# A third block of gate and up by seven products, and down with both column halves open, in a two-block transformer kernel on one Trainium2 core

## The chip, the core and the metric

The kernel runs on one core of one Trainium2 chip. The metric is the device time of one execution in microseconds, the median of several runs. The engines are named as in the profile: TensorE (PE, its weight loads PEld), VectorE (DVE), ScalarE (ACT), GpSimd (POOL) and SyncE (SP), which only issues DMAs.

## What is computed

Two transformer blocks on 256 tokens of width 1024, all in float32. The first block is a feed-forward stage, a mixer (top-k sparse attention beside a pooled branch) and a feed-forward stage; the second is a feed-forward stage, a gated mixer and a feed-forward stage, with a norm at the end. Cut to what the change touches:

```python
def swiglu(x, w_gate, w_up, w_down):          # w_gate, w_up 1024 x 2816; w_down 2816 x 1024
    return (jax.nn.silu(x @ w_gate) * (x @ w_up)) @ w_down

x = x + 0.5 * swiglu(rms_norm(x, g), w_gate, w_up, w_down)     # four times in all

q = rope(rms_norm(q.reshape(B, S, 8, 64), q_norm), pos, 64)    # first mixer; k likewise

return rmsnorm(x, final_norm)                                  # the end
```

## The kernel before

**Products.** Each float32 operand is split into a high and a low half that TensorE takes at full rate: ScalarE writes the high half (`whi`, L80), DVE subtracts it for the low half (`wlo`, L81). `mm3` (L83) makes one product of three matmuls: high by high (L86), high by low (L87), low by high (L88). A weight block is 128 x 2048 numbers, four k-tiles by 512 columns, 1 MB. It is loaded by SP's queue into one of two `raw` buffers or by POOL's queue into one of four `block` buffers of the stage, and split into one of three `whi`/`wlo` pairs. A block is used by 24 matmuls (2 token tiles x 4 k-tiles x 3), in the order of the token tiles.

**A feed-forward stage** (`ffn`, L322) has gate and up in six column blocks j = 0 to 5, the last one half as wide. `eight(j)` (L348) makes a block of gate and of up from four weight blocks, 96 matmuls. `seven(j)` (L362) makes the same by seven products of 12 matmuls each (`quad`, L157): four of the weight blocks' sums and differences are made, two by accumulating DMAs (L178), two on DVE (L196, L199, at the sixth and the seventh product), and the results are put together from the products by additions on DVE (L191, L197, L202 to L205, L367). The products go to the three PSUM banks of `tmp`. Every seven loads four weight blocks and accumulates two, splits seven, and takes all four `block` buffers in turn.

Behind a block come silu (L334) and the product with up (L342); `turned` (L208) then transposes it on TensorE and splits it into `act`, the operand of down.

`down` (L372) makes the two column halves f = 0 and 1 of the output one after the other, each over 22 k-tiles in five weight blocks (c = 0 to 4) and one of half size (c = 5). `add` (L254) puts a half into X, takes the squares for the next norm, and queues the transposes of X (L274) and the two halves of `hT` (L226, L227), the operand of the next stage; `later` and `flush` place them some steps on.

**Order.** `ORDER` (L36) is a string with a letter for each step of a stage, behind block 0: `a` and `b` are products of the two sevens (7 each), `2` and `4` the weight blocks of the two eights (4 each), `e` those of the half block (2), `d` those of down. The order of instructions on an engine, and the waits, are made by a scheduler from this order and the tiles' uses, so neighbours on an engine can change places.

**Elsewhere.** In the first mixer `mixer1_tables` (L426) loads constants and the gains `q_norm` and `k_norm` and makes with them on DVE the rope tables of q and k (L440, L443). `heads` (L520) uses these later. Behind the last stage, `run` (L853 to L870) loads the final gain `fg`, sums the squares, takes the inverse root on POOL (L101), multiplies and stores.

Of the kernel before, what the change touches and what calls it, by code (L numbers as in the profile page):

```python
# [10 lines left out]
F32 = mybir.dt.float32  # L11
F32R = mybir.dt.float32r
AF = mybir.ActivationFunctionType
ALU = mybir.AluOpType
# [3 lines left out]
P = 128  # L18
T = 256
D = 1024  # L20
KD = D // P
FF = 2816
KF = FF // P
HD = 64
NH = 8
# [7 lines left out]
MASKED = -1.0e30  # L33
WARM = 14

ORDER = "eeaa2a2aa2a2a44bb4b4bbdbdbdddddddddd"  # L36


class Block:
# [214 lines left out]
    def add(self, accs, f, scale, following, tiles=(0, 1)):  # L254
# [23 lines left out]
        for k in (4 * f, 4 * f + 2):  # L278
            self.later(lambda k=k: pair(k), 3)


    def warm_up(self):

# [38 lines left out]
    def ffn(self, n, following, first=False):  # L322
        nc, a = self.nc, self.a
        gu, d, d_end = a[f"gu{n}"], a[f"d{n}"], a[f"de{n}"]
        with self.stage(4), self.tc.tile_pool(name="act", bufs=1) as pool:
            act = pool.tile([P, KF, 2, T], F32R, tag="act", name="act")
            xc = pool.tile([P, 16, 2, P], F32R, tag="xc", name="xc")
            r = None

            def silu(gs):  # L330
                sgs = []
                for t in range(2):
                    sg = self.work.tile([P, 512], F32, tag="sg", name="sg")[:, : gs[t].shape[1]]
                    nc.scalar.activation(sg, gs[t], AF.Silu, scale=r[:, t : t + 1])  # L334
                    sgs.append(sg)
                return sgs

            def gated(j, sgs, us):
                prs = []
                for t in range(2):  # L340
                    pr = self.work.tile([P, 512], F32, tag="pr", name="pr", bufs=4)[:, : us[t].shape[1]]
                    nc.vector.scalar_tensor_tensor(pr, us[t], r[:, t : t + 1], sgs[t], op0=ALU.mult, op1=ALU.mult)  # L342
                    prs.append(pr)
                self.later(lambda: self.turned(act, prs, 4 * j), 4)

            two = lambda: [self.bank("acc") for _ in range(2)]

            def eight(j):  # L348
                G = two()
                self.token_major(G, gu[2 * j], 512, 0)  # L350
                yield
                self.token_major(G, gu[2 * j], 512, 1)
                sgs = silu([x[:, :T] for x in G] if j == 5 else G)
                if j < 5:
                    yield
                    U = two()
                    self.token_major(U, gu[2 * j + 1], 512, 0)
                    yield
                    self.token_major(U, gu[2 * j + 1], 512, 1)
                gated(j, sgs, [x[:, T:] for x in G] if j == 5 else U)  # L360

            def seven(j):  # L362
                y11, y21, y12, x, y22 = yield from self.quad(pool, [[gu[2 * j + i, c] for i in range(2)] for c in range(2)], self.hT, xc)

                def rest():
                    tt = nc.vector.tensor_tensor
                    tt(y12, y12, x, op=ALU.add)  # L367
                    gated(j, silu([y11, y21]), [y12, y22])

                self.later(rest, 3)  # L370

            def down():  # L372
                for f in range(2):
                    accs = two()
                    w = lambda c: self.weights(d[f, c] if c < 5 else d_end[f])
                    rows = lambda c, w, last, **k: self.rows(accs, w, act, 4 * c, 4 if c < 5 else 2, last, **k)
                    split = f == 1 and following == "final_norm_2"
                    order = (0, 1, 2, 4, 5, 3) if f == 0 else range(4 if split else 6)
                    for c in order:
                        if f or c:  # L380
                            yield
                        rows(c, w(c), 15 if f == 0 else KF - 1)
                    if split:
                        ws = [w(4), w(5)]
                        for t in range(2):
                            for c in (4, 5):
                                rows(c, ws[c - 4], KF - 1, tiles=[t])
                            self.add(accs, f, 0.5, following, [t])
                    else:
                        self.add(accs, f, 0.5, following)  # L390


            G, U = two(), two()
            if first:
                self.cold_start((G, U), gu)
            else:
                self.token_major(G, gu[0], 512, 0)
                self.flush()
                self.token_major(U, gu[1], 512, 0)
                self.flush()  # L400
                self.token_major(G, gu[0], 512, 1)
            r = self.rstd()
            if not first:
                self.token_major(U, gu[1], 512, 1)
            gated(0, silu(G), U)
            combined = self.combined(xc, self.hT)
            next(combined)

            steps = {"a": seven(1), "b": seven(3), "2": eight(2), "4": eight(4), "e": eight(5), "d": down()}
            for step in ORDER:  # L410
                next(steps[step], None)
                self.flush(1 if step in "ab" else 2)
                next(combined, None)

    def rope(self, dst, src, C, S, heads, half):
# [10 lines left out]
    def mixer1_tables(self):  # L426
        nc, a, c1 = self.nc, self.a, self.c1
        load = lambda name, shape, engine=None: self.load(c1, name, shape, engine)
        self.cosi, self.sini = load("cosi", [P, 2, 32]), load("sini", [P, 2, 32])
        cosq, sinq = load("cosq", [P, 2, 64]), load("sinq", [P, 2, 64])  # L430
        self.causal, self.ncausal = load("causal", [P, 2, T], nc.gpsimd), load("ncausal", [P, 2, T], nc.gpsimd)
        self.band, self.pw = load("band", [P, 4, 384], nc.gpsimd), load("pool_w", [P, 4, P], nc.gpsimd)
        self.pscale = load("pool_scale", [P, 4], nc.gpsimd)
        self.tabs = {}
        for n in ("q", "k"):
            g = c1.tile([P, HD], F32, tag=f"{n}g", name=f"{n}g")
            nc.sync.dma_start(g, a[f"{n}_norm"].to_broadcast([P, HD]))
            C = c1.tile([P, 2, HD], F32, tag=f"{n}C", name=f"{n}C")
            S = c1.tile([P, 2, HD], F32, tag=f"{n}S", name=f"{n}S")
            nc.vector.tensor_tensor(C, cosq, g[:, None, :].to_broadcast([P, 2, HD]), op=ALU.mult)  # L440
            for i in range(2):
                o, s = slice(i * 32, i * 32 + 32), slice(32 - i * 32, 64 - i * 32)
                nc.vector.tensor_tensor(S[:, :, o], sinq[:, :, o], g[:, None, s].to_broadcast([P, 2, 32]), op=ALU.mult)  # L443
            self.tabs[n] = (C, S)

    def mixer1(self, following):
        nc, a = self.nc, self.a
# [71 lines left out]

        def heads(n):  # L520
            rs, ros = [], []
            for t in range(2):
                src = accs[n][t].rearrange("p (h d) -> p h d", d=HD)
                ss = self.small.tile([P, NH], F32, tag="ss8", name="ss8")
# [3 lines left out]
                r = self.small.tile([P, NH], F32, tag=f"r8{n}", name="r8")  # L528
                self.rsqrt(r, ss, rr[:, t : t + 1])
                ro = self.m1.tile([P, NH, HD], F32, tag="ro", name="ro", bufs=2)  # L530
                self.rope(ro, src, self.tabs[n][0][:, t, :], self.tabs[n][1][:, t, :], NH, 32)
                nc.vector.tensor_scalar(r, r, rt[:, t : t + 1], HD ** -0.5 if n == "q" else 1.0, op0=ALU.mult, op1=ALU.mult)
                if n == "k":
                    for h in range(NH):
# [298 lines left out]
    def run(self):  # L833
# [16 lines left out]
            self.mixer2("ffn2_norm_2")  # L850
        self.ffn(4, "final_norm_2")

        fg = self.raw.tile([P, 2048], F32, tag="raw", name="fg")[:, :D]  # L853
        nc.sync.dma_start(fg, a["final"].to_broadcast([P, D]))
        for t in range(2):
            y = self.raw.tile([P, 2048], F32, tag="raw", name="y")[:, :D]
            tot = self.small.tile([P, 1], F32, tag="tot1", name="tot")
            nc.vector.tensor_tensor(tot, self.sq[:, 0, t : t + 1], self.sq[:, 1, t : t + 1], op=ALU.add)
            r = self.small.tile([P, 1], F32, tag="r1", name="r1")
            self.rsqrt(r, tot, 1.0 / D)  # L860
            for f in range(2):
                s = slice(f * 512, f * 512 + 512)
                nc.vector.tensor_tensor(y[:, s], self.X[t][:, s], fg[:, s], op=ALU.mult)
            for f in range(2):
                s = slice(f * 512, f * 512 + 512)
                if f:
                    nc.vector.tensor_scalar(y[:, s], y[:, s], r, None, op0=ALU.mult)
                else:
                    nc.scalar.activation(y[:, s], y[:, s], AF.Copy, scale=r)
                (nc.scalar if f == 0 and t == 1 else nc.sync).dma_start(self.out[t * P : t * P + P, s], y[:, s])  # L870

def _constants():
# [92 lines left out]
```

## Time and profile before

| what | us |
|---|---|
| median of 3 runs | 1085.7 (1085.14 to 1086.57) |
| the profiled execution | 1086.12 |
| its span in the trace | 1084.3 |
| TensorE busy | 1064.9 |
| DVE busy | 758.4 |
| ScalarE busy | 576.4 |

All times of the trace are microseconds from the span's start. Matmuls are pipelined: how long one takes says less than how far apart two of them start. "Idle before" is the time for which an engine had nothing to do before an instruction, followed by who ended it. The granted clock (PEclk) is the share of TensorE's full clock. The stages lie in the trace so: feed-forward up to 192 us, first mixer to 297, feed-forward to 479, feed-forward to 662, second mixer to 894, feed-forward to 1075, the end.

### The profile page before, as it was taken

How to read it: one execution, taken by the hardware profiler on the slowest of the kernel's cores; microseconds unless marked ns; L12 is line 12 of the kernel's file. 1: busy time of each engine (PE TensorE's matmuls, PEld its weight loads, DVE VectorE, ACT ScalarE, POOL GpSimd, SP SyncE). 2: the span in 40 equal slices, each digit the busy share in tenths (PEclk: the TensorE clock that was granted, in tenths of full speed). 3: DMA queues.
4: the chain of work that ended last, by engine and by line, in shares of the span. 5: the costliest groups of instructions: out<-in, count | busy, mean ns of one | idle time of the engine just before them, and what ended most of it. 6: DMA issues, size and time to landing. Idle time of an engine off the chain costs nothing.

```text
span 1084.3 us, 12898 instructions
## 1 busy us (share of the span) xinstructions
PE 1064.9 (98%) x5182; PEld 893.0 (82%) x5182; DVE 758.4 (70%) x780; ACT 576.4 (53%) x657; POOL 51.0 (5%) x85
## 2 busy tenths in 40 slices
PE   9899999899999999999999999999999999999996
PEld 8688888778888888888888878999888888888885
DVE  7788874697586969547788665777555467796953
ACT  7656543577456564545656345534444445556541
POOL 0100000120010000001000000000000001000000
PEclk9999999899999999999999999999999999999998
DMA  9976365633298643559773655454455438865361
GB/s 356 328 238 206 117 233 191 236 117 118 89 321 250 251 138 142 207 193 337 245 233 117 253 204 204 160 204 174 171 186 194 155 126 301 271 239 150 130 217 61
DMA packets 34955, 218.54 MB, mean 202 GB/s; under 512 B 4608, under 2 KB 5008, under 8 KB 10320
## 3 DMA queue, kind: packets, MB, share of 16 engines
q1 hardware_dynamic: 26784, 164.20, 41.4%
q0 software_dynamic: 7680, 52.98, 16.7%
q8 instruction: 40, 0.66, 0.2%
q10 hardware_dynamic: 432, 0.55, 0.1%
q14 instruction: 19, 0.16, 0.0%
HBM read 216.66 MB, written 1.05 MB: 201 GB/s over the span
## 4 chain that ended last, share of the span: by engine, by line
PE 92%; DMA 5%; DVE 1%; ACT 1%; issue 1%; SPq 0%; POOLq 0%; POOL 0%; ACTq 0%; DVEq 0%
PE acc L88 21%; PE acc L87 21%; PE acc L86 20%; PE tmp L86 8%; PE tmp L88 8%; PE tmp L87 8%; PE tmp L214 2%; DMA raw<-in_gu 1%; PE acc L94 1%; DMA block<-in_gu 1%; DVE wlo L81 1%; DMA qg<-in_q_norm 1%; DMA raw<-in_de 1%; PE tmp L274 1%; PE tmp L94 1%
## 5 line engine op out<-in xcount | busy, mean ns | idle before, releaser
L81 DVE TENSOR_TENSOR wlo<-raw,whi 128x2048 fp32r<-128x2048 f32 (+1 forms) x127 | 282.2, 2222 | 157.2 <-ACT whi L80 156.9
L80 ACT ACTIVATE whi<-raw 128x2048 fp32r<-128x2048 f32 (+1 forms) x127 | 236.5, 1862 | 210.9 <-PE acc L88 123.7
L81 DVE TENSOR_TENSOR wlo<-block,whi 128x2048 fp32r<-128x2048 f32 (+2 forms) x99 | 198.8, 2014 | 71.4 <-ACT whi L80 71.4
L80 ACT ACTIVATE whi<-block 128x2048 fp32r<-128x2048 f32 (+2 forms) x99 | 167.2, 1694 | 118.7 <-PE acc L88 59.9
L87 PE MATMUL acc<-wlo,hT 128*128 128x512 f32 (+1 forms) x560 | 218.6, 390 | 3.3 <-DVE wlo L81 3.3
L88 PE MATMUL acc<-whi,hT 128*128 128x512 f32 (+1 forms) x560 | 218.0, 390 | 3.2 <-DVE hT L227 3.2
L86 PE MATMUL acc<-whi,hT 128*128 128x512 f32 (+1 forms) x560 | 218.8, 392 | 0.0
L86 PE MATMUL acc<-whi,act 128*128 128x512 f32 x352 | 138.3, 393 | 0.6 <-ACT whi L80 0.5
L87 PE MATMUL acc<-wlo,act 128*128 128x512 f32 x352 | 136.9, 390 | 0.4 <-DVE wlo L81 0.4
L88 PE MATMUL acc<-whi,act 128*128 128x512 f32 x352 | 135.9, 389 | 0.0
L87 PEld LDWEIGHTS acc<-wlo,hT 128*128 128x128 f32 x560 | 106.1, 189 | 25.5 <-DVE wlo L81 4.4
L88 PEld LDWEIGHTS acc<-whi,hT 128*128 128x128 f32 x560 | 106.1, 189 | 24.6 <-DVE hT L227 3.5
L86 PEld LDWEIGHTS acc<-whi,hT 128*128 128x128 f32 x560 | 106.2, 190 | 21.9 <-ACT hT L226 0.5
L86 PEld LDWEIGHTS acc<-whi,act 128*128 128x128 f32 x352 | 66.1, 188 | 15.1 <-ACT act L80 1.3
L87 PEld LDWEIGHTS acc<-wlo,act 128*128 128x128 f32 x352 | 66.1, 188 | 14.8 <-DVE wlo L81 1.5
L88 PEld LDWEIGHTS acc<-whi,act 128*128 128x128 f32 x352 | 66.1, 188 | 13.9
L86 PE MATMUL tmp<-whi,hT 128*128 128x512 f32 x192 | 75.8, 395 | 0.0
L88 PE MATMUL tmp<-whi,hT 128*128 128x512 f32 x192 | 74.8, 390 | 0.0
L87 PE MATMUL tmp<-wlo,hT 128*128 128x512 f32 x192 | 74.8, 389 | 0.0
L86 PE MATMUL tmp<-whi,xc 128*128 128x512 f32 x128 | 50.2, 392 | 1.0 <-ACT p L175 1.0
L88 PE MATMUL tmp<-whi,xc 128*128 128x512 f32 x128 | 49.9, 390 | 0.0
L87 PE MATMUL tmp<-wlo,xc 128*128 128x512 f32 x128 | 49.8, 389 | 0.0
(264 smaller groups left out, 1380.0 us busy)
## 6 DMA issues: line engine op xcount, KB each, us to landing
raw<-in_gu SPq DMA_DIRECT2D x52, 1024.0 KB, 6.7
block<-in_gu POOLq DMA_DIRECT2D x48, 1024.0 KB, 8.3
raw<-in_d SPq DMA_DIRECT2D x40, 1024.0 KB, 4.8
raw<-in_de SPq DMA_DIRECT2D x8, 512.0 KB, 3.5
block<-in_w_out SPq DMA_DIRECT2D x4, 1024.0 KB, 4.9
raw<-in_w_out SPq DMA_DIRECT2D x4, 1024.0 KB, 5.6
block<-in_w_cx SPq DMA_DIRECT2D x4, 1024.0 KB, 5.0
raw<-in_w_cx SPq DMA_DIRECT2D x4, 1024.0 KB, 5.0
```

The source lines that it names most:

```text
L80: self.nc.scalar.activation(hi, x, AF.Copy)
L81: self.nc.vector.tensor_tensor(lo, x, hi.bitcast(F32), op=ALU.subtract)
L86: mm(ps, lhsT=a[0], rhs=b[0], start=start, stop=False)
L87: mm(ps, lhsT=a[0], rhs=b[1], start=False, stop=False)
L88: mm(ps, lhsT=a[1], rhs=b[0], start=False, stop=stop)
L94: self.nc.tensor.matmul(ps, lhsT=a, rhs=b, start=start, stop=stop)
L214: self.nc.tensor.transpose(pt[:, i, :], x[t][:, i * P : i * P + P], self.ident)
L274: nc.tensor.transpose(pt[:, i, t * P : t * P + P], self.X[t][:, (k + i) * P : (k + i) * P + P], self.ident)
```

## The change

In every feed-forward stage block 2 is made by seven products too, so that blocks 1, 2 and 3 are `a`, `b` and `c`, and the eights are 0, 4 and the half block. `ORDER` starts with the half block and block 4 among `a`, then puts blocks of down among `b` and `c`. For this `down` opens both column halves at once (four PSUM banks) and goes through the weight blocks in the order `DOWN`, pairs of half and k-block: k-blocks 0, 5 and 4 of both halves first, then 1, 2 and 3. The last weight block is done by token tile. The half f = 0 is added to X at the block before the last.

The rope tables of q and k are made on DVE in `heads`, where they are used; their loads stay where they were. The end loads `fg` and multiplies the first column half with it when that half is ready, makes half of the variance ahead, and does the rest of each token tile behind its part of the last weight block, with both queues for the stores.

```diff
-ORDER = "eeaa2a2aa2a2a44bb4b4bbdbdbdddddddddd"
+ORDER = "eeaa4aa4a4aa4bbdbbdbbdbccdccdcdcdcdddddd"
+DOWN = ((0, 0), (0, 5), (0, 4), (1, 0), (1, 5), (1, 4), (0, 1), (1, 1), (0, 2), (1, 2), (0, 3), (1, 3))
...
+    def ending(self):
...
+        self.fg = self.block()[:, :D]
+        nc.sync.dma_start(self.fg, self.a["final"].to_broadcast([P, D]))
+        self.half = self.small.tile([P, 2], F32, tag="tot", name="half")
+        nc.vector.tensor_scalar(self.half, self.sq[:, 0, :], 1.0 / D, EPS, op0=ALU.mult, op1=ALU.add)
+        self.y = [self.block()[:, :D] for _ in range(2)]
+        for t in range(2):
+            nc.vector.tensor_tensor(self.y[t][:, :512], self.X[t][:, :512], self.fg[:, :512], op=ALU.mult)
+
+    def finish(self, t):
+        nc, y = self.nc, self.y[t]
+        v = self.small.tile([P, 1], F32, tag="tot1", name="v")
+        nc.vector.scalar_tensor_tensor(v, self.sq[:, 1, t : t + 1], 1.0 / D, self.half[:, t : t + 1], op0=ALU.mult, op1=ALU.add)
+        r = self.small.tile([P, 1], F32, tag="r1", name="r1")
+        nc.gpsimd.tensor_tensor(r, v, self.mhalf[:, :1], op=ALU.pow)
+        nc.vector.tensor_tensor(y[:, 512:], self.X[t][:, 512:], self.fg[:, 512:], op=ALU.mult)
+        nc.scalar.activation(y[:, :512], y[:, :512], AF.Copy, scale=r)
+        nc.vector.tensor_scalar(y[:, 512:], y[:, 512:], r, None, op0=ALU.mult)
+        for f, queue in ((0, nc.scalar), (1, nc.sync)):
+            s = slice(f * 512, f * 512 + 512)
+            queue.dma_start(self.out[t * P : t * P + P, s], y[:, s])
...
-                self.later(lambda: self.turned(act, prs, 4 * j), 4)
+                self.later(lambda: self.turned(act, prs, 4 * j), 2 if j == 3 else 4)
...
             def down():
...
+                accs = [two(), two()]
+                for f, c in DOWN:
+                    if (f, c) != DOWN[0]:
+                        yield
+                    w = self.weights(d[f, c] if c < 5 else d_end[f])
+                    rows = lambda tiles: self.rows(accs[f], w, act, 4 * c, 4 if c < 5 else 2, 15, tiles=tiles)
+                    if (f, c) != DOWN[-1]:
+                        rows((0, 1))
+                        if c == 3:
+                            self.add(accs[f], f, 0.5, following)
+                            if following == "final_norm_2":
+                                self.ending()
+                        continue
+                    for t in range(2):
+                        if t:
+                            yield
+                        rows([t])
+                        if following == "final_norm_2":
+                            self.add(accs[f], f, 0.5, following, [t])
+                            self.finish(t)
+                    if following != "final_norm_2":
+                        self.add(accs[f], f, 0.5, following)
...
-            steps = {"a": seven(1), "b": seven(3), "2": eight(2), "4": eight(4), "e": eight(5), "d": down()}
+            steps = {"a": seven(1), "b": seven(2), "c": seven(3), "4": eight(4), "e": eight(5), "d": down()}
             for step in ORDER:
                 next(steps[step], None)
-                self.flush(1 if step in "ab" else 2)
+                self.flush(1 if step in "abc" else 2)
...
-        self.tabs = {}
+        self.heads_of = {}
         for n in ("q", "k"):
...
-            nc.vector.tensor_tensor(C, cosq, g[:, None, :].to_broadcast([P, 2, HD]), op=ALU.mult)
...
+            self.heads_of[n] = (cosq, sinq, g)
+
+    def tables_of(self, n):
...
         def heads(n):
             rs, ros = [], []
+            C, S = self.tables_of(n)
```

## Rows read from the trace of the kernel before

**Rows 1.** The page's first part: busy time, share of the span, instructions of each engine.
```profile
PE 1064.9 (98%) x5182; PEld 893.0 (82%) x5182; DVE 758.4 (70%) x780; ACT 576.4 (53%) x657; POOL 51.0 (5%) x85
```

**Rows 2.** Timeline of TensorE (start, us, what): first matmuls of two neighbouring products of b.
```profile
404.64 0.39 PE L86 MATMUL tmp<-whi,hT 128*128 128x512 f32 x1
...
407.36 0.39 PE L86 MATMUL tmp<-whi,xc 128*128 128x512 f32 x1
```

**Rows 3.** The list of TensorE's waits: us in total, times, longest us; the two largest.
```profile
PE acc L87 <- DVE wlo L81: 3.7, 3, 1.7
PE acc L88 <- DVE hT L227: 3.2, 1, 3.2
```

**Rows 4.** Table of stretches of the second feed-forward stage: us, busy us of each engine.
```profile
core 0: us, PE busy (x) PEld busy (x) DVE busy (x) ACT busy (x) POOL busy (x), PEclk, DMA share, GB/s
303.00:330.00 27.00, 27.00 (x122) 22.33 (x121) 21.65 (x18) 15.42 (x14) 4.03 (x7) 1.00 1.01 353
405.00:430.00 25.00, 25.00 (x116) 20.78 (x115) 23.88 (x19) 13.92 (x11) 0.00 (x0) 1.00 0.30 106
```

**Rows 5.** Timeline of DVE in that stretch, operations one behind the other.
```profile
404.70 2.28 DVE L196 TENSOR_TENSOR block<-block 128x2048 f32<-128x2048 f32 x1
...
407.56 0.68 DVE L191 TENSOR_TENSOR p<-tmp,p 128x512 f32<-128x512 f32 x1
408.16 2.28 DVE L81 TENSOR_TENSOR wlo<-raw,whi 128x2048 fp32r<-128x2048 f32 x1
410.36 2.29 DVE L81 TENSOR_TENSOR wlo<-block,whi 128x2048 fp32r<-128x2048 f32 x1
```

**Rows 6.** Timeline of TensorE: first use of the low half that started at 408.16.
```profile
411.19 0.40 PE L87 MATMUL acc<-wlo,act 128*128 128x512 f32 x1
```

**Rows 7.** The page's DMA issues: count, KB each, us from issue to landing.
```profile
block<-in_gu POOLq DMA_DIRECT2D x48, 1024.0 KB, 8.3
```

**Rows 8.** Timeline of TensorE: the transposes of X's first column half, second stage.
```profile
453.09 1.03 PE L274 MATMUL tmp<-ident,X 128*128 128x128 f32 x8
```

**Rows 9.** Timeline of DVE: the low halves of `hT` made from them.
```profile
457.45 0.87 DVE L227 SCALAR_TENSOR_TENSOR hT<-tmp,gains,hT 128x256 fp32r<-128x256 f32 x2
458.47 0.88 DVE L227 SCALAR_TENSOR_TENSOR hT<-tmp,gains,hT 128x256 fp32r<-128x256 f32 x2 [0.15 <-ACT hT L226]
```

**Rows 10.** Timeline of DVE in the first mixer: the first table and the next low half.
```profile
201.43 0.29 DVE L440 TENSOR_TENSOR qC<-cosq,qg 128x128 f32<-128x128 f32 x1 [4.54 <-DMA qg<-in_q_norm]
...
202.39 2.28 DVE L81 TENSOR_TENSOR wlo<-raw,whi 128x2048 fp32r<-128x2048 f32 x1
```

**Rows 11.** Timeline of TensorE in the first mixer: bounds of w_idx's two weight blocks.
```profile
191.54 0.31 PE L86 MATMUL acc<-whi,hT 128*128 128x324 f32 x1
...
195.10 1.04 PE L274 MATMUL acc<-ident,X 128*128 128x128 f32 x8
...
201.46 0.31 PE L86 MATMUL acc<-whi,hT 128*128 128x324 f32 x1
...
211.12 0.39 PE L86 MATMUL tmp<-whi,hT 128*128 128x512 f32 x1
```

**Rows 12.** Table of stretches, columns as in rows 4: the stop there and behind it.
```profile
201.40:205.10 3.70, 0.52 (x3) 0.21 (x2) 3.67 (x9) 0.00 (x0) 0.00 (x0) 0.83 0.98 406
205.10:210.60 5.50, 5.48 (x19) 5.24 (x20) 4.04 (x8) 3.19 (x4) 0.00 (x0) 0.50 0.63 220
```

**Rows 13.** Timeline of DVE in the tail, second token tile.
```profile
1076.74 0.16 DVE L858 TENSOR_TENSOR tot<-sq 128x1 f32<-128x1 f32 x1 [0.85 <-ACT junk L233]
...
1077.64 0.15 DVE L100 TENSOR_SCALAR var<-tot 128x1 f32<-128x1 f32 x1
1077.70 0.68 DVE L863 TENSOR_TENSOR y<-X,fg 128x512 f32<-128x512 f32 x1
```

**Rows 14.** Timeline of POOL in the tail: the inverse roots of both token tiles.
```profile
1073.10 0.56 POOL L101 TENSOR_TENSOR r<-var,mhalf 128x1 f32<-128x1 f32 x1 [94.69 <-DVE var L100]
1077.86 0.93 POOL L101 TENSOR_TENSOR r<-var,mhalf 128x1 f32<-128x1 f32 x1 [4.21 <-DVE var L100]
```

More of the change, by code (lines that the diff above doesn't have):

```diff
@@ L279, in add @@
             self.later(lambda k=k: pair(k), 3)
+    def ending(self):
+        nc = self.nc
+        self.fg = self.block()[:, :D]
[17 more added lines that the diff above has]
+            queue.dma_start(self.out[t * P : t * P + P, s], y[:, s])
     def warm_up(self):
@@ L372, in down @@
             def down():
[L373 to L380, printed above, removed]
-                            yield
[L382 to L390, printed above, removed]
+                accs = [two(), two()]
[13 more added lines that the diff above has]
+                        if t:
+                            yield
+                        rows([t])
[4 more added lines that the diff above has]
+                        self.add(accs[f], f, 0.5, following)
             G, U = two(), two()
@@ L437, in mixer1_tables @@
             nc.sync.dma_start(g, a[f"{n}_norm"].to_broadcast([P, HD]))
-            C = c1.tile([P, 2, HD], F32, tag=f"{n}C", name=f"{n}C")
-            S = c1.tile([P, 2, HD], F32, tag=f"{n}S", name=f"{n}S")
-            nc.vector.tensor_tensor(C, cosq, g[:, None, :].to_broadcast([P, 2, HD]), op=ALU.mult)
[L441 to L444, printed above, removed]
+            self.heads_of[n] = (cosq, sinq, g)
+    def tables_of(self, n):
+        nc, (cosq, sinq, g) = self.nc, self.heads_of[n]
+        C = self.c1.tile([P, 2, HD], F32, tag=f"{n}C", name=f"{n}C")
+        S = self.c1.tile([P, 2, HD], F32, tag=f"{n}S", name=f"{n}S")
+        nc.vector.tensor_tensor(C, cosq, g[:, None, :].to_broadcast([P, 2, HD]), op=ALU.mult)
+        for i in range(2):
+            o, s = slice(i * 32, i * 32 + 32), slice(32 - i * 32, 64 - i * 32)
+            nc.vector.tensor_tensor(S[:, :, o], sinq[:, :, o], g[:, None, s].to_broadcast([P, 2, 32]), op=ALU.mult)
+        return C, S
     def mixer1(self, following):
@@ L530, in heads @@
                 ro = self.m1.tile([P, NH, HD], F32, tag="ro", name="ro", bufs=2)
-                self.rope(ro, src, self.tabs[n][0][:, t, :], self.tabs[n][1][:, t, :], NH, 32)
+                self.rope(ro, src, C[:, t, :], S[:, t, :], NH, 32)
                 nc.vector.tensor_scalar(r, r, rt[:, t : t + 1], HD ** -0.5 if n == "q" else 1.0, op0=ALU.mult, op1=ALU.mult)
@@ L851, in run @@
         self.ffn(4, "final_norm_2")
[L853 to L870, printed above, removed]
 def _constants():
```

## The prediction

> **What bounds the kernel now.** I read the page's busy shares first: TensorE is busy 98% of the span, VectorE (DVE) 70% [rows 1]. Matmuls are pipelined, so a busy share alone proves little; the start times settle it. Twelve matmuls of 512 columns, one product of the seven, start 2.72 us apart from the next product's twelve [rows 2]: 0.227 us each, and a weight block of 24 takes 5.44 us. The list of TensorE's waits then adds to about 10 us in all; its two largest entries are 3.7 us on DVE's low halves (`wlo`) and one wait of 3.2 us on a low half of `hT` [rows 3]. So TensorE sets the time nearly everywhere, and a matmul taken out is worth its 0.227 us, if what feeds TensorE keeps up.
>
> What feeds it is DVE: each weight block needs its low half from DVE, and only three pairs `whi`/`wlo` exist, so a block's split can't start before the matmuls of the third block before it are done. The table of stretches shows the second feed-forward stage: at its densest, 405 to 430 us, DVE is busy 23.88 of 25.00 us while TensorE is busy throughout; from 303 to 330 us, near the stage's start, the DMA engines move 353 GB/s [rows 4].
>
> **1. Twelve matmuls fewer per stage.** A block of gate and up by eight products is 4 x 24 = 96 matmuls, by seven 7 x 12 = 84. One block more in four stages: 48 x 0.227 = **-10.9 us**, all on the path.
>
> **2. What the third seven adds on DVE.** Three more low halves, two more sums of weight blocks and some eight operations of 512 elements per stage. On a busy DVE, starts follow each other by 2.2 us (weight sum), 0.6 us (512 elements) and 2.2 us (low half) [rows 5]. Per stage 3 x 2.2 + 2 x 2.2 + 8 x 0.6 = 15.8 us; over a stage of some 180 us that fits. Where it falls is the question. I add up what DVE owes around the end of a seven, where its two weight sums, the sum at the sixth product, the five sums behind the seventh and the two gated products fall together:
> - Before, `b d b d b d` at the end of b: TensorE 3 x 2.72 + 3 x 5.44 = 24.5 us; DVE 6 x 2.2 + 2 x 2.2 + 8 x 0.6 + two halves of `act` 1.2 = 23.6 us. This is the stretch read as 23.88 of 25.00 [rows 4], so the bookkeeping holds.
> - After, `a a 4 b b d`: TensorE 4 x 2.72 + 2 x 5.44 = 21.8; DVE 6 x 2.2 + 4.4 + 10 x 0.6 (block 4's gated products come here too) = 23.6: 1.8 us too much.
> - After, `b d b c c d`: 21.8 against 13.2 + 4.4 + 4.8 = 22.4: 0.6 too much.
> - After, `c d c d`: 16.3 against 8.8 + 4.4 + 4.8 = 18.0: 1.7 too much, with six blocks of down behind it in which DVE recovers.
>
> Together 4.1 us per stage. Against it stands the lead. A block of 24 behind two products of 12 has the least: the low half that starts at 408.16 ends at 410.44 and its first matmul runs at 411.19, 0.75 us ahead [rows 5, 6]. There are four such places per stage before (`aa2` twice, `bb4`, `bbd`) and eight after (`aa4` three times, `bbd` three times, `ccd` twice). Other blocks are further ahead. So I let a third of the 4.1 through: 1.4 us per stage, **+5.5 us**; the ends are 0 (the lead swallows all) and 4 x 4.1 = 16.4. A gain is excluded, but for the few waits that TensorE has there now.
>
> The added DMAs: six per seven on GpSimd's queue, two of them accumulating behind another. A 1 MB block lands 8.3 us after its issue [rows 7]. The next seven's first block takes the buffer that the weight sum at the sixth product frees, so between issue and use lie at least the sixth product, a block of 24 and the seventh, 10.9 us, and the lead. During b the traffic is 9 MB in 35 us, about 260 GB/s, under the 353 moved elsewhere [rows 4]. I cost it at nothing; where the cover fails it is part of the upper end above.
>
> **3. Down with both halves open.** The number of matmuls stays. It holds four of five `acc` banks until the end, and the first column half of X is now ready one block before the end, not six. So its `hT` (four k-tiles) stands on the path into the next stage, which starts with them. Before, eight transposes start at 453.09 and the low halves of `hT` start at 457.45 and 458.47, two each, the first done 4.84 us and the last 6.26 us after the transposes' start [rows 8, 9]. After, behind them come only their own 1.03 us and the second tile's 2.72; the third matmul of the next stage needs the first low half 4.2 us after the transposes' start: 0.6 late, the last one at 6.2, just in time. DVE and ScalarE have the sums and squares of X to do there as well, so I take 1.0 us at each of three transitions (the last stage has none): **+3.0 us**, ends 0 (no weight split is put in between) and 4.5.
>
> **4. The rope tables.** The low halves of w_q, and those of `hT` for the second half of w_idx behind them, queue on DVE behind the tables, which wait for `q_norm`: DVE idles 4.54 us up to 201.43, and the next low half starts at 202.39 [rows 10]. TensorE stops soon after 201.46. The second part of idx takes from 201.46 to 211.12, 9.66 us; the same 24 matmuls of the first part took 191.54 to 195.10, 3.56 us [rows 11]. The difference, 6.1 us, is a stop and then 5.5 us at the lower clock level: granted share 0.50 from 205.1 to 210.6 [rows 12]. With the tables made in `heads` DVE goes on at 196.9: the low half (2.2 us) and the four of `hT` (1.8 us by [rows 9]) end near 201, just in time. The load stays where it is on SP's queue; nobody waits for it until the next group but one. The tables' 1 us moves into a stretch where DVE has the top-k rounds; so I take **-5.5 us**, ends -6.1 and -4.0.
>
> **5. The tail.** Behind the last square comes `tot` at 1076.74, but `var` only at 1077.64, because a product with `fg` stands between; pow runs from 1077.86 to 1078.79, and the scaling waits for it [rows 13, 14]. After, half of the sum is made ahead, so pow starts near 1076.95, 0.9 us sooner; one product with `fg` remains and runs beside pow. Pow took 0.56 us with DVE free and 0.93 beside such a product [rows 13, 14]. **-0.9 us**, ends -0.4 (the first tile's scale holds the second tile's X sum on DVE) and -1.3.
> The Trainium skill, "SBUF — State Buffer", section "SBUF: two separate sides", says that a DVE operation with two SBUF inputs and a GpSimd operation that reads SBUF lock each other out for a whole instruction. The two durations of pow agree with it in kind; by it pow stays at 0.93, since the product is still put beside it, which is what the term holds.
>
> **Sum.** -10.9 + 5.5 + 3.0 - 5.5 - 0.9 = -8.8 us. The profiled execution took 1086.1 us (span 1084.3 and 1.8 around it): 1077.3. The median of the runs is 0.4 lower: **1077 us**.
>
> **Rivals.**
> - *DVE keeps up*: no wait in step 2, little at the transitions, full gain at the tables: -10.9 + 1.0 - 6.1 - 1.2 = -17.2, 1068.5 us. For it: 23.88 of 25.00 passed without a wait [rows 4]. Against: twice as many places with 0.75 us of lead. 0.17.
> - *The tables' gain comes due elsewhere*: the top-k rounds on DVE behind it start sooner but end when they did, or TensorE meets another late input, and 5.5 us are lost again: 1082.5 us. For: DVE is densely used there. Against: TensorE hardly waits in that stretch now [rows 3]. 0.12.
> - *Slower: DVE's debt becomes stops that take the clock down.* Place: `a a 4 b b d` and `b d b c c d`. After the stop of 3.5 us the clock was at half for 5.5 us [rows 12], which cost some 2.5 us more. If the 4.1 us come through whole, once per stage with such a fall: 4 x 6.6 = 26.4, and -10.9 + 26.4 + 3.0 - 5.5 - 0.9 = +12.1, 1098 us. The rest of the sum is -14.3, so it decides from 3.6 us lost per stage on, and is measurably slower from 4.1. [...] 0.09.
> The Trainium skill, "TensorE: Matmul & The Clock Gate", section "HAM oscillation — how this bites in real kernels", describes such repeated falls behind waits for input. The granted 0.50 behind the stop agrees; in the feed-forward stretches of the table it is 1.00 [rows 4].
>
> **How the numbers follow.** The forecast (1070 to 1083) has 0.62, the rivals 0.17, 0.12 and 0.09. The range leaves out the slower rival and the far end of the first: 1068 to 1086. About 0.2% is what a measurement of this kernel can tell from no change, so faster means under 1083.5: 0.62 + 0.17 + a quarter of the second rival = 0.82; same 0.09; slower 0.09.
>
> **What would show it.** Right: 48 matmuls fewer; a granted clock of 1.00 from 195 to 215 us and no wait on `q_norm`; waits of TensorE on `wlo` of 0.3 to 1.5 us at the ends of a and b, and on `hT` at the start of the stages after the first. Wrong: waits of over 2 us there, a clock of 0.50 inside a feed-forward stage, TensorE waiting on a DMA into `block`, or DVE with spare time at the ends of the sevens.

## The result and the profile after

The changed kernel took **1112.3 us** (median of 4 runs, 1109.4 to 1115.3), the kernel before 1085.4 beside it: ratio 1.0248, 95% interval 1.0228 to 1.0268. The forecast was 1077 us in a range to 1086. The profiled execution took 1109.4 us, its span is 1107.7. The page's first part:

```profile
PE 1067.8 (96%) x5134; PEld 882.3 (80%) x5134; DVE 818.4 (74%) x827; ACT 605.3 (55%) x685; POOL 66.3 (6%) x109
```

The 48 matmuls are gone (5182 before [rows 1]). TensorE's busy share fell by two points. The page's chain that ended last says more. Its first line is the share of the span by engine, here of the kernel before, then of the changed one with a line of the costliest groups:

```profile
PE 92%; DMA 5%; DVE 1%; ACT 1%; issue 1%; SPq 0%; POOLq 0%; POOL 0%; ACTq 0%; DVEq 0%
```
```profile
PE 67%; DVE 17%; ACT 7%; issue 6%; DMA 3%; SPq 0%; ACTq 0%; POOLq 0%; POOL 0%; DVEq 0%
...
L82 ACT ACTIVATE whi<-block 128x2048 fp32r<-128x2048 f32 (+2 forms) x127 | 219.9, 1741 | 126.6 <-DVE block L201 55.7
```

DVE and ScalarE together carry 24% of the chain, 2% before. The group's line is ScalarE's rounding of weight blocks to high halves (line 80 of before is line 82 here, 81 is 83, 86 to 88 are 88 to 90, the two weight sums 196 and 199 are 198 and 201). The largest part of its idle time, 55.7 of 126.6 us, ends with a **weight sum on DVE** (`block`, line 201). TensorE's list of waits, against [rows 3] (us in total, times, longest):

```profile
PE acc L88 <- ACT whi L82: 13.4, 14, 1.8
PE tmp L88 <- ACT whi L82: 5.9, 4, 1.5
PE acc L89 <- DVE wlo L83: 4.3, 3, 2.2
PE acc L90 <- DVE hT L229: 2.6, 1, 2.6
```

The new waits are for *high* halves, which hardly any matmul waited for before. The prediction looked only at low halves.

**The place.** It is the second feed-forward stage, where the order is `b b d b b d b b d b`: products 5 and 6 of b stand side by side. ScalarE's timeline (start, us, what, in brackets the idle time before it and what ended it):

```profile
393.51 1.91 ACT L82 ACTIVATE whi<-block 128x2048 fp32r<-128x2048 f32 x1
...
400.66 1.91 ACT L82 ACTIVATE whi<-block 128x2048 fp32r<-128x2048 f32 x1 [1.56 <-DVE block L198]
```

DVE's timeline there:

```profile
395.45 2.29 DVE L83 TENSOR_TENSOR wlo<-block,whi 128x2048 fp32r<-128x2048 f32 x1 [2.53 <-ACT whi L82]
397.66 0.68 DVE L193 TENSOR_TENSOR p<-tmp,p 128x512 f32<-128x512 f32 x1
398.26 2.28 DVE L198 TENSOR_TENSOR block<-block 128x2048 f32<-128x2048 f32 x1
402.60 2.29 DVE L83 TENSOR_TENSOR wlo<-block,whi 128x2048 fp32r<-128x2048 f32 x1 [2.06 <-ACT whi L82]
```

and TensorE's:

```profile
400.75 0.39 PE L90 MATMUL tmp<-whi,xc 128*128 128x512 f32 x1
402.62 0.50 PE L88 MATMUL tmp<-whi,xc 128*128 128x512 f32 x1 [1.48 <-ACT whi L82]
404.90 0.50 PE L88 MATMUL acc<-whi,act 128*128 128x512 f32 x1 [1.78 <-ACT whi L82]
```

Read the three together as one chain in series. Product 5 rounds `w11` (1.91), takes its low half (2.29), and only then may the sum `w11 += w22` (2.28) overwrite `w11`, because both halves of product 5 read it. Product 6 then rounds the sum (1.91) and takes its low half (2.29), ready at 404.89. From 393.51 to 404.89 are 11.4 us, with 0.6 us of other work on DVE between. TensorE runs out of the work that its order allows it and stands twice: starts lie 1.87 and 2.28 us apart where 0.227 is the usual distance, the pitch. (The second stop ends with the high half of the block of down, which ScalarE could round only behind product 6's.) **DVE meanwhile is idle** for 2.53 and 2.06 us: not overloaded, but waiting in the same chain.

The same two stops, 1.64 and 2.06 us beyond the pitch, stand in all four stages (from 110.7, 400.75, 587.36 and 1011.52). In the first two the granted clock stays at 1.00, in the last two it falls to 0.50 behind them. Table of stretches (columns as in [rows 4]):

```profile
398.00:408.00 10.00, 6.74 (x29) 5.00 (x28) 7.94 (x5) 4.92 (x4) 0.55 (x1) 1.00 0.31 105
592.00:594.00 2.00, 2.00 (x6) 1.52 (x6) 2.00 (x2) 0.00 (x0) 0.00 (x0) 0.50 0.04 16
1015.80:1021.00 5.20, 5.20 (x13) 4.04 (x14) 4.35 (x2) 0.76 (x1) 0.31 (x1) 0.50 0.37 126
```

To size it, take each distance between the starts of two neighbouring matmuls, subtract the median distance of its form, and add up (half clock counts with the stops). Over the whole trace that is 22.2 us before and 55.6 after; from the first weight sums of a stage to the end of c, 0.5 to 0.6 us in each of the four stages before and 8.3, 8.2, 9.1 and 10.4 after. I call this **lost starts** below. The stages lost 34 us more than before, the matmuls gave back 10.9.

**The first table didn't move.** DVE in the first mixer, where [rows 10] showed an idle time of 4.54 us:

```profile
199.74 0.29 DVE L500 TENSOR_SCALAR rr<-rr 128x2 f32<-128x2 f32 x1
205.22 0.29 DVE L475 TENSOR_TENSOR qC<-cosq,qg 128x128 f32<-128x128 f32 x1 [5.19 <-DMA qg<-in_q_norm]
...
205.56 2.28 DVE L83 TENSOR_TENSOR wlo<-raw,whi 128x2048 fp32r<-128x2048 f32 x1
```

The source calls the tables later, but on DVE the first two of the six table operations still stand ahead of w_q's low half (only the others moved behind it), and the stop (TensorE's 2.6 us on `hT` in the list of waits) is the one of before.

### The profile page after: what moved, and what is told of

Its sections match the earlier page's. It is cut to its first block, busy times and chain, and to the rows that moved or that the text cites. A ratio compares the mean times of both kernels' runs of the same rounds, so it can differ in the third digit from the quotient of the medians.

```text
span 1107.7 us, 12935 instructions
## 1 busy us (share of the span) xinstructions
PE 1067.8 (96%) x5134; PEld 882.3 (80%) x5134; DVE 818.4 (74%) x827; ACT 605.3 (55%) x685; POOL 66.3 (6%) x109
## 4 chain that ended last, share of the span: by engine, by line
PE 67%; DVE 17%; ACT 7%; issue 6%; DMA 3%; SPq 0%; ACTq 0%; POOLq 0%; POOL 0%; DVEq 0%
PE acc L89 14%; PE acc L90 14%; PE acc L88 14%; DVE wlo L83 9%; PE tmp L89 7%; PE tmp L90 7%; PE tmp L88 7%; ACT whi L82 6%; DVE block L198 2%; DVE block L201 2%; PE acc L96 1%; PE tmp L216 1%; DMA xT<-in_xT 1%; DVE pr L368 1%; DMA raw<-in_d 1%
## 5 line engine op out<-in xcount | busy, mean ns | idle before, releaser
L83 DVE TENSOR_TENSOR wlo<-block,whi 128x2048 fp32r<-128x2048 f32 (+2 forms) x127 | 262.0, 2074 | 93.7 <-ACT whi L82 93.5
L83 DVE TENSOR_TENSOR wlo<-raw,whi 128x2048 fp32r<-128x2048 f32 (+1 forms) x111 | 245.5, 2212 | 110.7 <-ACT whi L82 110.5
L82 ACT ACTIVATE whi<-raw 128x2048 fp32r<-128x2048 f32 (+1 forms) x111 | 205.0, 1851 | 172.2 <-PE acc L90 78.6
L82 ACT ACTIVATE whi<-block 128x2048 fp32r<-128x2048 f32 (+2 forms) x127 | 219.9, 1741 | 126.6 <-DVE block L201 55.7
L88 PE MATMUL acc<-whi,hT 128*128 128x512 f32 (+1 forms) x432 | 168.0, 392 | 5.0 <-ACT whi L82 4.9
L89 PE MATMUL acc<-wlo,hT 128*128 128x512 f32 (+1 forms) x432 | 168.6, 390 | 2.5 <-DVE wlo L83 2.5
L90 PE MATMUL acc<-whi,hT 128*128 128x512 f32 (+1 forms) x432 | 167.3, 388 | 2.6 <-DVE hT L229 2.6
L88 PEld LDWEIGHTS acc<-whi,hT 128*128 128x128 f32 x432 | 81.4, 189 | 24.2 <-ACT whi L82 7.0
L90 PEld LDWEIGHTS acc<-whi,hT 128*128 128x128 f32 x432 | 81.6, 189 | 19.2 <-DVE hT L229 3.1
L88 PE MATMUL tmp<-whi,hT 128*128 128x512 f32 x240 | 94.3, 395 | 0.0
L90 PE MATMUL tmp<-whi,hT 128*128 128x512 f32 x240 | 93.6, 390 | 0.0
L88 PE MATMUL tmp<-whi,xc 128*128 128x512 f32 x192 | 77.1, 402 | 7.0 <-ACT whi L82 5.9
L89 PE MATMUL tmp<-wlo,xc 128*128 128x512 f32 x192 | 77.1, 401 | 0.0
L90 PE MATMUL tmp<-whi,xc 128*128 128x512 f32 x192 | 76.2, 397 | 0.0
```

Source lines behind the costliest of these rows:

```text
L82: self.nc.scalar.activation(hi, x, AF.Copy)
L83: self.nc.vector.tensor_tensor(lo, x, hi.bitcast(F32), op=ALU.subtract)
L88: mm(ps, lhsT=a[0], rhs=b[0], start=start, stop=False)
L89: mm(ps, lhsT=a[0], rhs=b[1], start=False, stop=False)
L90: mm(ps, lhsT=a[1], rhs=b[0], start=False, stop=stop)
```

## Experiments

Every kernel ran beside the kernel before on one chip; that had medians of 1084.8, 1083.8 and 1084.6 us in the three groups of runs (experiments 1 to 4; 5, 6, 7 and 9; 8, 10 and 11). The groups ran on three chips, so between groups the spans of the profiled executions and the lost starts stand beside the medians below.

**Theories.** *Chain*: neighbouring products 5, 6 and 7 of a block put rounding, low half and sum in series. *Debt* (the prediction's): DVE has too much to do at the ends of the sevens. They are told apart by the sum's destination, which leaves DVE's work as it is.

**1. Another order**, with a block of 24 matmuls between the neighbours.
```diff
-ORDER = "eeaa4aa4a4aa4bbdbbdbbdbccdccdcdcdcdddddd"
+ORDER = "eeaa4a4aa4a4abbdbdbbdbdbccdcccdcdcdddddd"
```


> The changed kernel with another ORDER alone: the same letters, but a weight block of 24 matmuls between the fifth, sixth and seventh product of each seven (a6 a7 and b5 b6 stood side by side). Chain theory: the weight sum for the sixth product writes into the buffer that the fifth product's split still reads, so split, sum and split stand one behind the other (1.9 + 2.3 + 2.3 + 1.9 + 2.3 us), and TensorE stops where only 2.7 us of matmuls lie between; without neighbours the stops of some 6.5 us per stage go: 1086 us. Debt theory (DVE simply owes too much work around the end of a seven): the work is the same, at most a third is gained back: 1104 us or more.


Measured: 1084.3 us, ratio 0.9996 (0.9987 to 1.0006). 28 us back, lost starts 3.5 us per stage. It fits the chain, but an order also spreads DVE's work, so it doesn't decide.

**2. The sums in buffers of their own**, in the changed kernel's order.
```diff
-        tt(w11, w11, w22, op=ALU.add)
-        tt(v, product(of_xc(1), self.parts(w11)), v, op=ALU.subtract)
+        tt(w22, w11, w22, op=ALU.add)
+        tt(v, product(of_xc(1), self.parts(w22)), v, op=ALU.subtract)
...
-        tt(w11, w11, w21, op=ALU.add)
-        w = self.parts(w11)
+        tt(w21, w22, w21, op=ALU.add)
+        w = self.parts(w21)
```


> The changed kernel with its ORDER, but the two weight sums are written into the buffer of the other summand (w22 at the sixth product, w21 at the seventh) and not into w11; every operation and its size stay. Chain theory: the sums no longer wait for the split of the product before, the stops at neighbouring products go: 1086 to 1092 us. Debt theory: nothing changes, 1108 to 1115 us.


Measured: **1075.3 us**, ratio 0.9912 (0.9897 to 0.9927), lost starts 0.9 to 1.1 us per stage. That is 11 us below what the chain was expected to be worth at best; the theory's sign was right, its size too small. `w22` and `w21` were last split for products 3 and 4, so a sum into them needn't wait for product 5's split. DVE at the same place of the order (b's products 5 and 6):

```profile
379.53 2.28 DVE L198 TENSOR_TENSOR block<-block 128x2048 f32<-128x2048 f32 x1
...
384.06 2.28 DVE L201 TENSOR_TENSOR block<-block 128x2048 f32<-128x2048 f32 x1
386.26 0.68 DVE L193 TENSOR_TENSOR p<-tmp,p 128x512 f32<-128x512 f32 x1
386.87 4.48 DVE L83 TENSOR_TENSOR wlo<-block,whi 128x2048 fp32r<-128x2048 f32 x2
391.27 2.28 DVE L83 TENSOR_TENSOR wlo<-raw,whi 128x2048 fp32r<-128x2048 f32 x1
```

Both sums are done before the low halves of 5 and 6, which follow each other at 2.2 us with no idle time. The same operations cost 37.0 us less (1112.3 to 1075.3; 35.9 by the spans, of which 32 are lost starts of the four stages and 3 those at the transition behind the third): the chain carries nearly all of the loss, and DVE's amount of work at most the 0.4 to 0.5 us per stage by which lost starts still exceed those of before.

**3. The half-open down and the tail without a third seven.**
```diff
-ORDER = "eeaa4aa4a4aa4bbdbbdbbdbccdccdcdcdcdddddd"
+ORDER = "eeaa2a2aa2a2a44bb4b4bbdbdbddddddddddd"
...
-            steps = {"a": seven(1), "b": seven(2), "c": seven(3), "4": eight(4), "e": eight(5), "d": down()}
+            steps = {"a": seven(1), "b": seven(3), "2": eight(2), "4": eight(4), "e": eight(5), "d": down()}
```


> The changed kernel with only two sevens per stage (block 2 by eight products) in the order of the kernel before; down with both halves open, the tables and the end stay changed. If the third seven and its order are all that costs: 1085 to 1089 us. If the half-open down costs by itself: above 1095 us.


Measured: 1082.7 us, ratio 0.9990 (0.9979 to 1.0000). TensorE's waits:

```profile
PE acc L89 <- DVE wlo L83: 3.5, 2, 1.8
PE acc L90 <- DVE hT L229: 2.7, 1, 2.7
```

The one wait on `hT` is that of the tables (it lies between 196 and 216 us). At the three transitions TensorE waits for no `hT`. What stands there is one stop of 2.1 us beyond the pitch behind the third stage, on a block of down that landed late; the kernel before has two there, of 0.65 and 0.58. The half-open down costs nothing measurable in the time.

**4. The tables on GpSimd.**
```diff
-        nc.vector.tensor_tensor(C, cosq, g[:, None, :].to_broadcast([P, 2, HD]), op=ALU.mult)
+        nc.gpsimd.tensor_tensor(C, cosq, g[:, None, :].to_broadcast([P, 2, HD]), op=ALU.mult)
...
-            nc.vector.tensor_tensor(S[:, :, o], sinq[:, :, o], g[:, None, s].to_broadcast([P, 2, 32]), op=ALU.mult)
+            nc.gpsimd.tensor_tensor(S[:, :, o], sinq[:, :, o], g[:, None, s].to_broadcast([P, 2, 32]), op=ALU.mult)
```


> The changed kernel with the rope tables made on GpSimd, not on DVE. If the wait for q_norm on DVE, still at its old place, is what stops TensorE at 205 us: 5 us faster than the changed kernel, 1107 us, and a granted clock of 1.00 behind it. If TensorE meets another late input there: 1111 to 1113 us.


Measured: 1108.6 us, ratio to before 1.0218 (1.0203 to 1.0234), 3.7 us under the changed kernel (3.5 by the spans). The table of stretches from 200 to 220 us, the changed kernel and then this one:

```profile
200.00:220.00 20.00, 17.33 (x80) 14.27 (x79) 12.92 (x30) 10.13 (x29) 1.73 (x3) 0.91 0.62 217
```
```profile
200.00:220.00 20.00, 19.32 (x109) 15.83 (x107) 14.92 (x33) 13.57 (x45) 5.47 (x10) 1.00 0.79 299
```

The stop is gone and the clock holds. Now GpSimd waits for `q_norm`, and nothing stands behind it that TensorE needs.

**5. Both causes removed** (the diffs of 2 and 4).


> The changed kernel with the sums for products 6 and 7 written into buffers that no split reads, and the rope tables on GpSimd. If the two causes stand in different places of the kernel they add: 1075.3 less the 3.7 us that the tables' move alone gave (1112.3 to 1108.6) = 1071.6, the stop at 198 to 205 us of the version with sums apart is gone and TensorE's clock holds there. Rival, the tables' gain comes due later (the products of q, k or v wait for something else, or the two GpSimd multiplications hold VectorE's port): 1074 to 1076, with a new wait between 200 and 240 us. Behind the last landing the end should again be 4.2 to 4.5 us away, since the DMAs issued on GpSimd's queue are 81 as in the changed kernel.


Measured: **1070.2 us**, ratio 0.9869 (0.9854 to 0.9885). The two add: for the tables 4.2 us here by the spans (1071.8 to 1067.7), 5.0 by the medians, which come from two chips. All that is left of TensorE's waits over half a microsecond:

```profile
PE acc L89 <- DVE wlo L83: 2.1, 2, 1.1
PE acc L90 <- DVE act L83: 1.1, 1, 1.1
PE tmp L96 <- POOL mhalf L874: 1.0, 1, 1.0
PE tmp L88 <- ACT p L177: 0.8, 3, 0.3
PE tmp L96 <- ACT rel L533: 0.7, 1, 0.7
```

**6. The same sums in the kernel before**, as a control: the diff of 2, nothing else.


> The kernel before, with the sums for products 6 and 7 written into other buffers as in the fast version, and nothing else changed. If the serial chain costs only where products 5, 6 and 7 of a block stand next to each other, which they never do in the order before, this is no change: 1085 (1084 to 1086). If writing the sums elsewhere were a gain in itself (fewer waits at other places, another order of VectorE), it would be some us faster, up to 8, and the gain of the version with sums apart would not be the change's own.


Measured: 1084.3 us, ratio 1.0001 (0.9989 to 1.0012). In the old order 5, 6 and 7 are never neighbours, and the sum's destination is worth nothing. The price comes from sums *and* order together.

**7. Only b and c put apart.**
```diff
-ORDER = "eeaa4aa4a4aa4bbdbbdbbdbccdccdcdcdcdddddd"
+ORDER = "eeaa4aa4a4aa4bbdbdbbdbdbccdcccdcdcdddddd"
```


> The changed kernel with the order put apart only behind block a: products 5 and 6 of the second and third block have another product or a whole block of down between them, products 6 and 7 of the first block stay next to each other. With all neighbours apart the time was 1084.3. If the chain's price is per place, the first block's own is about 1.2 to 2 us a stage (its gap of 1.19 us at 367 and what the clock loses behind it), so 1084.3 + 4 x 1.2 to 2 = 1089 to 1092; the rest of the 28 us, 20 or more, belongs to the second and third block's place. If the stop comes from how much VectorE has to do in the stage, wherever the products stand, it moves to another place and the time stays over 1100.


Measured: 1091.6 us, 7.4 over the first experiment by the medians, 8.7 by the spans (1089.9 and 1081.2). The place `a a` (products 6 and 7) loses 2.2 us of starts in each stage here and 0.1 in experiment 1. The rest, 20.7 us by the medians and 17.8 by the spans, came back with the new order of b and c. Products 5, 6 and 7 of c stand apart in the changed order already, so the neighbours among these are `b b` (products 5 and 6), with the two stops shown above. TensorE's waits from 340 to 450 us in this kernel:

```profile
PE acc L88 <- ACT whi L82: 1.0, 1, 1.0
PE tmp L88 <- DVE p L193: 0.6, 1, 0.6
PE tmp L88 <- ACT whi L82: 0.3, 1, 0.3
```
In the changed kernel, from 350 to 450 us, they were 4.3 us on `whi`, 1.8 the longest.

The price goes by place, and `b b` has the larger part.

**8. Both cures of the chain**: the order of 1 and the sums of 2.


> Both cures of the chain in one kernel: the order that puts products 5, 6 and 7 apart, and the sums in buffers of their own. The order alone gave 1084.3, the sums alone 1075.3, and the 9 us between them are open. If what was left with the order alone is the chain still (a sum that waits for a split, partly covered), the time is that of the sums alone, 1075 (1074 to 1077). If the new order has a price of its own, with another cause (more of VectorE's work where less of TensorE's covers it), it stays at 1080 to 1085, with the stops at 124, 136, 143 and 147 us still there.


Measured: 1080.6 us (1078.1 to 1081.7), ratio 0.9969 (0.9957 to 0.9982), between the two answers, so neither was right alone; lost starts 2.4 to 2.6 us per stage. Of the 9 us between 1 and 2, some 3.6 were chain, some 5.4 belong to the order itself. At the stop that is left (842 ns between two starts at 424.59) DVE has been busy without idle time from 415.80 on:

```profile
415.80 6.79 DVE L83 TENSOR_TENSOR wlo<-block,whi 128x2048 fp32r<-128x2048 f32 x3 [1.29 <-ACT whi L82]
422.50 2.29 DVE L198 TENSOR_TENSOR block<-block 128x2048 f32<-128x2048 f32 x1
424.70 0.68 DVE L193 TENSOR_TENSOR p<-tmp,p 128x512 f32<-128x512 f32 x1
425.30 1.28 DVE L83 TENSOR_TENSOR act<-tmp,act 128x512 fp32r<-128x512 f32 x2
426.49 2.28 DVE L83 TENSOR_TENSOR wlo<-raw,whi 128x2048 fp32r<-128x2048 f32 x1
```

That is what the predicted debt looks like: full DVE, small stops. It belongs to the order `d c c c d`, not to the changed kernel's. Whether it is the only cause of the 5.4 us wasn't tested.

**9. Where the tail's gain went.** Behind the last power on GpSimd (the inverse root of the end) the outputs land within 2.5 us of their issue in every kernel, but the span ended 5.5 us behind that power before and 7.8 after. What differs is the number of transfers issued on GpSimd's queue: 48 blocks of gate and up [rows 7] and nine others before, 72 and nine after. Here 24 of the loads go to SP's queue, in the kernel of 5.
```diff
-        w11, w22, w21 = self.block(b11), self.block(b22), self.block(b21)
+        w11, w22, w21 = self.block(b11), self.block(b22, nc.sync), self.block(b21, nc.sync)
```


> As the run with both causes removed, and two of the four plain loads of each group of blocks (24 loads in all) are issued on the SP queue in place of GpSimd's, so that GpSimd issues 57 DMAs as in the kernel before, not 81. What is under test is the kernel's end: GpSimd's last instruction ended 4.74 us behind the last power with 57 DMAs and 6.70 us with 81. If it goes by the number of DMAs, it ends about 4.7 us behind the power here, the end of the span stands 2.2 us behind the last landing in place of 4.4, and the kernel is 2 us faster than the run beside it: about 1069.5, if no load comes late. If it goes by something else (the kind of transfer, the accumulating ones above all, which stay on GpSimd), it stays at 6.7 and the end at 4.4. Loads on SP stand behind raw loads there, so a wait on a block or raw load of up to some us in a feed-forward stage would be a price of this edit and not of the end.


Measured: 1074.0 us, ratio 0.9904 (0.9888 to 0.9919). The end did what was expected, 5.5 us behind the power in place of 7.5. The time was lost at another place, in the first stage, where a raw load on SP stood behind the moved ones (SP's queue waited up to 7.9 us there for DVE to free a `block` buffer). ScalarE:

```profile
48.51 1.91 ACT L82 ACTIVATE whi<-raw 128x2048 fp32r<-128x2048 f32 x1 [4.70 <-DMA raw<-in_gu]
```

**10 and 11. The same from the second stage on**, with 18 and with all 36 plain loads of these stages.
```diff
+        self.quads = getattr(self, "quads", 0) + 1
+        queue = nc.sync if self.quads > 3 else nc.gpsimd
...
-        w11, w22, w21 = self.block(b11), self.block(b22), self.block(b21)
+        w11, w22, w21 = self.block(b11), self.block(b22, queue), self.block(b21, queue)
```
In the second of the two `b12` and `b11` go by `queue` too.


> As the run with 24 loads on SP, but only from the second feed-forward stage on: 18 loads go to SP, GpSimd issues 63 DMAs. The stop of 3.7 us at 46.5 us, in the first stage, where the raw load on SP stood behind the moved ones, should be gone, and with it the half clock behind it. If the end goes by the number of DMAs that GpSimd issued, at 2.0 us for 24 of them, the way from the last power's end to the span's end is 7.5 less 18 x 0.083 = 6.0 us, and the time 1070.2 - 1.5 = 1068.7. Rival: it goes by the kind of DMA or by a step (at 57 or 60, say): 5.5 or 7.5 us, and 1068.2 or 1070.2.

> As the run beside it, with all four plain loads of a group on SP from the second stage on: 36 loads, GpSimd issues 45 DMAs. By the number: 7.5 less 36 x 0.083 = 4.5 us from the last power to the end, 3 us less than with 81, while the outputs land some 3.3 us behind the power, so that the end stands close to the landing: 1067.2. If something else then ends last (the wait for the landing itself), the way stays near 5 us: 1067.7. If the loads on SP hold back raw loads, a stop of 1 to 4 us stands in stages 2 to 4, and it is no faster than 1070.


Measured: 1068.7 us, ratio 0.9858 (0.9843 to 0.9872), **the fastest kernel here**; and 1085.5 us, ratio 1.0009 (0.9998 to 1.0019), where four waits of up to 3.0 us on `whi` stand in TensorE's list (raw loads held back again: SP's queue waited up to 7.6 us for a `block` buffer around 500 us). The ends, GpSimd's last power and the span's last instant, for the changed kernel, 5 and 11 in this order (the head of an answer gives the span):

```profile
core 0 of [0], span 1107.7 us
...
1099.34 0.55 POOL L299 TENSOR_TENSOR r<-v,mhalf 128x1 f32<-128x1 f32 x1 [2.18 <-DVE v L297]
```
```profile
core 0 of [0], span 1067.7 us
...
1059.62 0.54 POOL L299 TENSOR_TENSOR r<-v,mhalf 128x1 f32<-128x1 f32 x1 [2.18 <-DVE v L297]
```
```profile
core 0 of [0], span 1083.3 us
...
1078.20 0.55 POOL L301 TENSOR_TENSOR r<-v,mhalf 128x1 f32<-128x1 f32 x1 [2.18 <-DVE v L299]
```

From the power's end: 7.8 and 7.5 us with 81 transfers, 6.0 with 63 (experiment 10), 4.6 with 45, and 5.5 with 57, both before [rows 14] and in experiment 9. From 81 to 45, experiment 5 to 11, that is 2.9 us for 36, 0.08 us each.

## Why the prediction was wrong

**What bounds it.** Right for the kernel before: with the chain cut and the tables moved TensorE sets the time again (99% busy in the fastest kernel). The clause "if what feeds TensorE keeps up" held the whole case.

**Step 1, -10.9 us: right.** 48 matmuls fewer. The third seven with the chain cut (experiment 2) against the same kernel without it (experiment 3): lost starts are 20.0 and 19.9 us, and experiment 2 ends 2.0 us later behind the last power. -10.9 + 0.1 + 2.0 = -8.8; the spans of the two are 1071.8 and 1080.7, -8.9.

**Step 2, +5.5 us with ends 0 and 16.4: this is the step that failed.** The step had +5.5; the four stages lost 33.9 us more than before. Cutting the chain (experiment 2) gave back 37.0 us by the medians, 35.9 by the spans. The bookkeeping set DVE's *amount* of work against TensorE's, place by place, and let a lead of 0.75 us absorb part. It never asked which operation must follow which: that the sum writes into the buffer whose split is just being read. The product, the sum and the low half were in [rows 2, 5], the rounding (1.9 us) in the same trace: 1.9 + 2.3 + 2.3 + 1.9 + 2.3 = 10.7 us in series against 2.72 us for a product, or 8.2 with a block of 24 between. The kernel before has the chain too, from 399.89 (rounding for product 5 of b) to the end of the last low half of [rows 5] at 412.65, and TensorE runs through it without a stop, because a block of 24, products 4 and 5 and the next block of 24 lie beside it. The step even listed new neighbours (`aa4`, `bbd`, `ccd`), but as places with a small lead for a block of 24, not as places where a sum has nothing to hide behind; these are the last `a a` (products 6 and 7) and the last `b b` (5 and 6). Its upper end, 4 x 4.1, was the whole of DVE's excess and so no bound on a latency. DVE's debt itself, where it does show (experiment 8), costs stops of under a microsecond. In the changed order with the sums apart it is at most 0.4 to 0.5 us per stage over before.

**Step 3, +3.0 us: the wait on `hT` isn't there** (experiment 3). Its lower end, 0, was right for that wait. One transition of the changed kernel does show a stop, after the third stage, but for a transfer: a 1 MB block of down landed 9.66 us after its issue at 644.5, beside the mixer's loads, and TensorE waited 1.8 us for its low half and then ran at half clock (PEclk 0.89 over 655 to 670). That lost 4.4 us of starts, against 1.7 before and 2.5 in experiment 3; the fastest kernels have a stop of 1.1 to 1.2 us there. The step had no such term.

**Step 4, -5.5 us: the mechanism was right, the edit doesn't do it.** Taking the tables out of DVE's way is worth 3.5 us in experiment 4 and 4.2 in experiment 5 by the spans (3.7 and 5.0 by the medians); in the changed kernel lost starts from 196 to 216 us are 4.7, against 6.2 before. The prediction took the place in the source for the place on the engine. None of its rivals had the tables staying where they were.

**Step 5, -0.9 us: a gain swallowed.** From the last sum into X to the last landing it is 1.3 us shorter than before, but not quite as predicted. The product with `fg` ran ahead of `v`, beside ScalarE's squares, and not beside pow:

```profile
1098.32 0.69 DVE L300 TENSOR_TENSOR block<-X,block 128x512 f32<-128x512 f32 x1
1099.10 0.16 DVE L297 SCALAR_TENSOR_TENSOR v<-sq,half 128x1 f32<-128x1 f32 x1
```

So pow starts 1.74 us behind the start of the last sum into X (2.66 before), the 0.9 us of the step, and takes 0.55 us in place of 0.93 [rows 14]. Then the end came 2.2 us later behind pow (7.8 in place of 5.5), with 24 more transfers on GpSimd's queue; the step had no term for that.

**The sum again**, from the spans, 1107.7 - 1084.3 = +23.4 (the median of the runs of the changed kernel is 2.9 us above its profiled execution; the other three have a mean granted clock of 0.984 to 0.988, the profiled one 0.989): -10.9 for the matmuls; +33.9 lost starts in the four stages; -0.5 lost starts elsewhere (tables and transitions); -1.3 and +2.2 in the tail. Together +23.4.

**The rivals.** The slower one had places, sign and the half clock behind a stop right, at 0.09 and 1098 us. But its mechanism, DVE's debt, isn't what happened. Its fall of the clock came in two stages of four, behind two stops of 1.6 and 2.1 us beyond the pitch with one matmul between them, and cost about 1 and 2 us there. In the other two the clock held behind the same stops (1.00 from 398 to 408), and the price was over 8 us of lost starts all the same; why it fell in two and not in all isn't shown. The first rival, *DVE keeps up* at 1068.5 us, is what the same change gives once sums, tables and GpSimd's issues are put right (1068.7), though that is another kernel than the one forecast.

**The signs named.** "A clock of 0.50 inside a feed-forward stage" and "DVE with spare time at the ends of the sevens" had been named as signs of a wrong prediction, and both stand in the trace. The waits at the ends of a and b stayed under the 2 us named (1.8 the longest) and were for high halves.

## What to carry to other kernels

Adding up an engine's work in a stretch bounds throughput only; for each buffer that is rewritten in place, write out the chain of operations from its last readers to the next use and set its length against what the bottleneck has to do in between. Before two steps are made neighbours, ask what hid between them, and give an in-place sum another dead buffer as its target when one is at hand (here four changed lines gave back 37 us). Look for an operation's place on its engine in the trace, not in the source.

## What was not expected of the hardware

The end of the span came the later the more transfers GpSimd had issued in the whole kernel, though the last of them had landed long before: 4.6 us behind its last instruction with 45, 5.5 with 57, 6.0 with 63, 7.5 to 7.8 with 81 (GpSimd's next recorded instruction comes after 6.7 us in both, so these 0.3 us arise behind it). Loads moved to SP's queue don't count. The trace doesn't show what GpSimd does in that time.
